# A transformer block on one core: the order of two engines at the start of the feed-forward's first pass, and a separate place for four loads of its last stage

## The chip, the cores and the metric

The kernel runs on one core of one Trainium2 chip. The core has a matrix engine (PE, with its weight loads PEld beside it), a vector engine (DVE), a scalar engine (ACT), a general engine (POOL) and SyncE (SP), which here only issues transfers (DMAs). Each engine takes its instructions in the order in which they are written and waits for the others by semaphores. The metric is the time of one execution on the device in microseconds (us), lower is better.

## The reference, cut to what matters

All inputs are float32; one sequence of 2048 rows of width 1024 passes through one block. The change lies in the second half of the block, the feed-forward, and at the boundary to it.

```python
def reference(x, c, w_cond, ..., w_out, g_ffn_pre, g_ffn_post, w_gate, w_up, w_down):
    ...                                   # attention and pooling give mix
    x = x + gate_m * rmsnorm(mix, g_mix_post)
    h = rmsnorm(x, g_ffn_pre) * (1.0 + scale_f) + shift_f
    f = (silu(h @ w_gate) * (h @ w_up)) @ w_down      # 1024 -> 2816 -> 1024
    return x + gate_f * rmsnorm(f, g_ffn_post)
```

## The kernel before, in words

Rows are held in 16 tiles of 128 rows, and the 2816 inner columns in 22 chunks of 128. A float32 product is made of three products of a rounded high part and a low part (`mm3`, L69 to L74: high by high on L72, the two mixed ones on L73 and L74). So an operand must be split before PE can use it: ACT casts the high part, DVE subtracts it from the operand and keeps the low part. In the down stage this is `split` (L62 on ACT, L63 on DVE). In the first passes it is `split_by_bank` (L1169 to L1177): ACT casts, ACT copies the rounded part to a PSUM bank (`rounded`), and DVE subtracts from there.

The feed-forward products are made by a scheme of seven products in place of eight (two levels for gate and up, one level for down). Four first passes p1 to p4 hold 11 blocks each. A block, `inner(q, j)`, has seven products with the names a, e, f, b, h, i and d, of six matmuls each. The order on PE is a, e, f, b, h, i of the first block, then a of the next, d of the first, e, f, b, h, i of the next, and so on. The weights of a block arrive as `g` and `u`; POOL makes the sums `s12` and `s34` of their parts; `g`, `s12`, `s34` and `u` are then split. Each of these splits, and each product, is a step with a number: e of the second block is step 8, its split of `s12` belongs to that step. What a product leaves in PSUM is taken up by DVE: `u2p` (L1410) from f, `p_c` (L1396) from b, `u3p` (L1418) from h, then `p_c` from e, from i and from d. Products d and e share two PSUM banks in turn (`e_ps`), so e of a block can only start when the `p_c` that reads the e of the block before has ended. `u4p` goes by ACT (L1406) and POOL (L1414).

While the first pass starts, the last tile of rows (number 15) still passes the boundary: DVE adds the input to it (L1272, 128x1024), ACT squares it and sums (L1255), DVE and POOL make the factor (`fr_v` L124, `fr_r` L126), and DVE and ACT scale one half each (`x1s`, L1266 and L1267). PE then transposes it (`f_pt`, L135) after h of the second block.

The order on PE, ACT, DVE and POOL is the order in which this loop writes the instructions; `n` counts the steps, `end_of_rows(n)` runs right after the products of a step, `split_up_to(n)` makes the splits of the steps ahead (up to six operand pairs), and `takes` are the DVE and ACT steps that take up results. SP's order is not written by hand: the compiler's scheduler places each transfer by when its tile is free. A transfer waits in SP's queue for all that stand before it.

The down stage works twice (`down(0)` and `down(1)`, for 1024 rows each) through the seven products p1, p2, p6, p7, p5, p4 and p3, each over 11 chunks, with 12 matmuls per chunk. The left operands (`g0p`, `g1p`) come from DRAM in groups of four chunks (three in p1), as two tiles of two chunks, and the groups take the pools `ring` and `fx` in turn; the right ones (`w0p`, `w1p`) come four chunks at a time. A tile can be loaded again when the splits of what it held are done. Products are split three chunks ahead, since there are six operand pairs. Results leave as `out_dram`; `x1b` and `cr` are the rows and first halves that are added at the end.

The tag `sr` names four tiles of 128x512 in pool `fx`. They serve the gate-and-up stage, and nothing uses them in the down stage.

## Time and profile before

| | |
|---|---|
| median of the runs, us | 2198.0 |
| lowest run, us | 2197.82 |
| profiled execution, us | 2196.93 |
| its span, us | 2195.1 |
| PE busy in the span | 99% |
| DVE, ACT, POOL busy | 76%, 62%, 55% |
| mean granted PE clock | 0.999 |

The span runs from the first to the last instruction of the profiled execution; 1.8 us of its time lie around it. The first pass starts at 983 us of the span, the first `down` at about 1767 us, and the second at 1976 us. A timeline row gives start and duration in us, engine, line, operation, out<-in, and in square brackets the idle time of the engine just before, with what ended it. PE's rows overlap: the next matmul starts before the one before has ended, so the pace is read from the starts.

### The profile page before, as it was taken

The numbers are of one execution on the slowest core, as the hardware profiler recorded it, in microseconds if no ns is written. First come the engines' busy times: TensorE is split into PE (matmuls) and PEld (weight loads), VectorE is DVE, ScalarE is ACT, GpSimd is POOL, SyncE is SP. The second block draws the span as 40 slices with busy tenths as digits, with TensorE's granted clock in tenths as the row PEclk, the third lists the DMA queues.
The fourth block names the chain that finished last, engine by engine and source line by source line (L and its number), as shares of the span: only waits on it lengthen the run. The fifth ranks groups of instructions, "written<-read, shape, count | busy, mean of one in ns | idle before, by whom it ended". The sixth has DMA issues, their size and how long they took to land.

```text
span 2195.1 us, 34256 instructions
## 1 busy us (share of the span) xinstructions
PE 2170.2 (99%) x10349; PEld 1795.4 (82%) x10349; DVE 1679.1 (76%) x2552; ACT 1356.9 (62%) x2796; POOL 1216.9 (55%) x1700
## 2 busy tenths in 40 slices
PE   8999999999999999999999999999999999999998
PEld 5888888888888888887888888888888888887887
DVE  7874499999999967647777878788778765576566
ACT  5335589989989855547666667654445444455454
POOL 1352277787879966537787877656666520032003
PEclk9999999999999999999999999999999999999999
DMA  9996886634343545668889989999999897589553
GB/s 315 338 294 208 284 215 177 172 90 120 111 137 95 154 163 199 218 197 284 285 299 314 310 267 293 292 327 327 304 300 303 304 333 256 196 261 316 187 198 118
DMA packets 365573, 524.78 MB, mean 239 GB/s; under 512 B 24198, under 2 KB 203978, under 8 KB 357836
## 3 DMA queue, kind: packets, MB, share of 16 engines
q1 hardware_dynamic: 360476, 518.13, 72.2%
q10 hardware_dynamic: 4912, 4.46, 0.7%
q8 instruction: 82, 1.34, 0.3%
q14 instruction: 103, 0.84, 0.1%
HBM read 350.01 MB, written 172.49 MB: 238 GB/s over the span
## 4 chain that ended last, share of the span: by engine, by line
PE 90%; DVE 4%; ACT 2%; POOL 2%; issue 1%; DMA 1%; SPq 0%; DVEq 0%; POOLq 0%; ACTq 0%
PE wt L964 4%; PE dn0p L74 3%; PE dn0p L72 3%; PE dn0p L73 3%; PE mix L74 3%; PE mix L72 3%; PE mix L73 3%; PE dn1p L73 2%; PE dn1p L72 2%; PE dn1p L74 2%; PE av L980 2%; PE z L929 2%; PE z L930 2%; PE av L979 2%; PE t_u L73 2%; PE t_g L73 2%
## 5 line engine op out<-in xcount | busy, mean ns | idle before, releaser
L953 POOL TENSOR_TENSOR w<-sg,pr 128x512 f32<-128x512 f32 (+2 forms) x320 | 306.6, 958 | 46.3 <-DVE pr L948 14.8
L948 DVE TENSOR_TENSOR_SCAN pr<-pr,carry,begin 128x512 f32<-128x512 f32 x192 | 244.0, 1271 | 0.0
L932 ACT ACTIVATE sg<-z 128x512 f32<-128x512 f32 (+2 forms) x320 | 183.1, 572 | 51.0 <-PE z L930 41.1
L63 DVE TENSOR_TENSOR wtl<-wt,wth 128x512 fp32r<-128x512 f32 (+1 forms) x320 | 189.5, 592 | 17.9 <-ACT wth L62 15.9
L62 ACT CAST wth<-wt 128x512 fp32r<-128x512 f32 (+1 forms) x320 | 181.8, 568 | 10.4 <-PE wt L964 8.1
L934 ACT ACTIVATE pr<-z 128x512 f32<-128x512 f32 (+2 forms) x320 | 182.1, 569 | 0.0
L964 PE MATMUL wt<-ident,w 128*128 128x128 f32 x1088 | 172.3, 273 | 1.6 <-POOL pr L944 1.1
L964 PEld LDWEIGHTS wt<-ident,w 128*128 128x128 f32 x1088 | 134.1, 140 | 32.8 <-POOL pr L944 1.9
L1493 ACT ACTIVATE sa<-sa 128x512 f32<-128x512 f32 x88 | 54.8, 632 | 164.7 <-DVE sa L1492 164.7
L979 PE MATMUL av<-wth,vt 128*128 128x512 f32 (+1 forms) x320 | 126.1, 394 | 0.9 <-ACT o L984 0.8
L63 DVE TENSOR_TENSOR g0p_l<-g0p,g0p_h 128x512 fp32r<-128x512 f32 x77 | 59.6, 774 | 79.7 <-ACT g0p_h L62 79.7
L72 PE MATMUL dn0p<-w0p_h,g0p_h 128*128 128x512 f32 x308 | 119.8, 389 | 0.0
L73 PE MATMUL dn0p<-w0p_l,g0p_h 128*128 128x512 f32 x308 | 119.8, 389 | 0.0
L74 PE MATMUL dn0p<-w0p_h,g0p_l 128*128 128x512 f32 x308 | 119.8, 389 | 0.0
L929 PE MATMUL z<-kt,qt 128*128 128x512 f32 (+2 forms) x320 | 118.7, 371 | 0.7 <-ACT pr L934 0.6
L980 PE MATMUL av<-wtl,vt 128*128 128x512 f32 (+1 forms) x320 | 117.8, 368 | 1.3 <-DVE wtl L63 1.2
L930 PE MATMUL z<-kt,qt 128*128 128x512 f32 (+2 forms) x320 | 116.9, 365 | 0.0
L72 PE MATMUL dn1p<-w1p_h,g1p_h 128*128 128x512 f32 x292 | 113.7, 389 | 0.6 <-ACT w1p_h L62 0.6
L73 PE MATMUL dn1p<-w1p_l,g1p_h 128*128 128x512 f32 x292 | 113.8, 390 | 0.3 <-DVE w1p_l L63 0.3
L74 PE MATMUL dn1p<-w1p_h,g1p_l 128*128 128x512 f32 x292 | 113.6, 389 | 0.0
L62 ACT CAST g0p_h<-g0p 128x512 fp32r<-128x512 f32 x77 | 48.0, 623 | 105.3 <-PE dn0p L73 89.3
L945 DVE TENSOR_TENSOR_SCAN pr<-pr,zero,begin 128x128 f32<-128x128 f32 (+3 forms) x128 | 111.1, 870 | 1.7 <-ACT pr L934 1.7
(852 smaller groups left out, 7155.9 us busy)
## 6 DMA issues: line engine op xcount, KB each, us to landing
pd<-p_c SPq DMA_DIRECT2D x176, 256.0 KB, 4.6
px<-pd SPq DMA_DIRECT2D x42, 1024.0 KB, 7.3
hs<-h2d SPq DMA_DIRECT2D x71, 256.0 KB, 4.8
wc<-in_w_cond_dram SPq DMA_DIRECT2D x32, 512.0 KB, 7.6
qt<-qd SPq DMA_DIRECT2D x64, 256.0 KB, 4.0
kt<-kd SPq DMA_DIRECT2D x96, 128.0 KB, 3.3
vt<-vd SPq DMA_DIRECT2D x48, 256.0 KB, 3.8
wd<-in_w_down_dram SPq DMA_DIRECT2D x44, 256.0 KB, 5.6
```

Source lines behind the costliest of these rows:

```text
L62: nc.scalar.copy(hi, src)
L63: low.tensor_tensor(lo, src, raw(hi), ALU.subtract)
L72: nc.tensor.matmul(ps, lh, rh, start=first and i == 0, stop=False)
L73: nc.tensor.matmul(ps, lh, rl, start=False, stop=False)
L74: nc.tensor.matmul(ps, ll, rh, start=False, stop=last and i == n - 1)
L929: nc.tensor.matmul(z[:, 0:L], qt[:, 0, i * P:(i + 1) * P], keys, start=True, stop=False)
L932: nc.scalar.activation(sg[:, 0:L], z[:, 0:L], AF.Sigmoid, scale=0.125)
L934: nc.scalar.activation(pr[:, 0:L], z[:, 0:L], AF.Sigmoid, scale=-0.125)
L948: nc.vector.tensor_tensor_scan(keys, keys, begin, carry, ALU.mult, ALU.bypass)
L953: nc.gpsimd.tensor_tensor(w[:, 0:L], sg[:, 0:L], pr[:, 1:L + 1], ALU.mult)
L964: nc.tensor.transpose(wt[:, i * P:(i + 1) * P], wss[u][i][:, b * P:(b + 1) * P], ident)
L979: nc.tensor.matmul(av[:, lo0:], vb, wh[:, lo0:], start=first, stop=False)
```

## The change

Three places are edited.

First, after step 1 of the main loop the splits are made up to and with step 8 before the last tile of rows is squared. So ACT's cast and copy of the second block's first `s12` and DVE's low part of it come ahead of the square and of what follows it.

Second, the scaling of the last tile of rows (with the closing of a pool and the opening of `ops0b`, which stand beside it) moves from `end_of_rows(4)` to the end of the body of step 5, behind the sums that take up b and e of the first block.

Third, in `down(1)` the first four chunks of the left operand of product p2 no longer go to the tiles of `ring` and `fx`, but to the four `sr` tiles, as four loads of 256 KB in place of two of 512 KB, and they are written eight steps ahead in place of five. Since this group no longer counts in the turn of the two pools, each later group of `down(1)` uses the other pool than before.

```diff
             def chunk(j):
                 name = f"{sb}{n}_{j}"
+                early = sb and n == "p2" and not j
 
                 def load_g():
                     m = min(QF, HF - held - j)
+                    if early:
+                        ph["gq", 0] = [ft("sr", f"g{name}_{i}") for i in range(m)]
+                        for i, t in enumerate(ph["gq", 0]):
+                            nc.sync.dma_start(t, ga[sb][a][:, i, :])
+                        return
                     quads.append(j)
                     ph["gq", j // QF] = t = raw_pair(ring if len(quads) % 2 else fx, f"g{name}", (P, 2, TB))
...
                 def split_gw():
                     pairs = []
-                    for kind, s in (("g", ph["gq", j // QF][j % QF // 2][:, j % QF % 2, :]), ("w", ph["w", j // 4][:, j % 4])):
+                    quad = ph["gq", j // QF]
+                    g = quad[j % QF] if len(quad) > 2 else quad[j % QF // 2][:, j % QF % 2, :]
+                    for kind, s in (("g", g), ("w", ph["w", j // 4][:, j % 4])):
...
                 if j % QF == 0:
-                    s.ahead.append((8 if begin else 5, load_g))
+                    s.ahead.append((8 if begin or early else 5, load_g))
...
     def end_of_rows(n):
         if n == 0:
             add_last_x(*last_rows)
-        if n == 4:
-            late.append((SEQUENCE[-1], last_scale[1](last_scale[2])))
-            op2st.close()
-            opools["0b"] = open_pool(h2st, "ops0b")
...
         if n == 1:
+            while split_to < 9:
+                steps[split_to].split()
+                split_to += 1
             last_scale.extend(ffn_rows(SEQUENCE[-1], *last_rows))
         if n == 3:
             last_scale.append(last_scale[0]())
+        if n == 5:
+            late.append((SEQUENCE[-1], last_scale[1](last_scale[2])))
+            op2st.close()
+            opools["0b"] = open_pool(h2st, "ops0b")
         next_side()
```

The order on PE and POOL stays as it was. Place one is DVE at the start of the first pass, right after the 128x1024 addition to the last rows (`x_15`); `p_1_g_l` and `p_1_s_l` are low parts of the second block's weights, `p_0_c` and the `u` names are what the first block's products leave. Before:

```order
L1177 TENSOR_TENSOR p_1_g_l<-p_1_321_13015,rounded 128x512
L1410 TENSOR_TENSOR u2p_0_13129<-fp_0_13113,p1p_0_13106 128x512
L1177 TENSOR_TENSOR p_1_s_l<-p_1_s_13087,rounded 128x512
L124 TENSOR_SCALAR fr_v<-s_15_13108 128x1
L1266 TENSOR_SCALAR x1s_13149<-x_15_13046,fr_r 128x512
L1396 TENSOR_TENSOR p_0_c_13157<-bp_0_13122,p1p_0_13106 128x512
L1418 TENSOR_TENSOR u3p_0_13173<-hp_0_13142,u2p_0_13129 128x512
L1396 TENSOR_TENSOR p_0_c_13175<-ep_0_13093,u3p_0_13173 128x512
```

And DVE at the same place with the change:

```order
L1177 TENSOR_TENSOR p_1_g_l<-p_1_321_13015,rounded 128x512
L1177 TENSOR_TENSOR p_1_s_l<-p_1_s_13087,rounded 128x512
L1410 TENSOR_TENSOR u2p_0_13135<-fp_0_13119,p1p_0_13106 128x512
L124 TENSOR_SCALAR fr_v<-s_15_13114 128x1
L1396 TENSOR_TENSOR p_0_c_13149<-bp_0_13128,p1p_0_13106 128x512
L1418 TENSOR_TENSOR u3p_0_13165<-hp_0_13142,u2p_0_13135 128x512
L1396 TENSOR_TENSOR p_0_c_13167<-ep_0_13093,u3p_0_13165 128x512
L1266 TENSOR_SCALAR x1s_13169<-x_15_13046,fr_r 128x512
```

The low part of `s12` moved one place ahead of `u2p`, and the scaling `x1s` moved from ahead of the three sums on b, h and e to behind them. ACT at the same place, as one piece of the difference, from the copy of the first block's product a (`p1p_0`) on; `m` and `s_15` are what the square writes:

```order
 L1401 COPY p1p_0_13106<-ap_0_13078 128x512
-L1255 ACTIVATE m_11480,s_15_13108<-x_15_13046 128x1024
-L1406 COPY u4p_0_13120<-ep_0_13093 128x512
 L1169 CAST p_1_s_h<-p_1_s_13087 128x512
 L1176 COPY rounded<-p_1_s_h 128x512
-L1267 ACTIVATE x1s_13149<-x_15_13046,fr_r 128x512
-L1169 CAST p_1_s_h<-p_1_s_13110 128x512
+L1255 ACTIVATE m_11480,s_15_13114<-x_15_13046 128x1024
+L1406 COPY u4p_0_13126<-ep_0_13093 128x512
+L1267 ACTIVATE x1s_13169<-x_15_13046,fr_r 128x512
+L1169 CAST p_1_s_h<-p_1_s_13116 128x512
```

On ACT the cast and the copy of `s12` moved ahead of the square and of `u4p`. Place two is SP's queue late in product p1 of `down(1)`, with the loads for p2 (`g1p2`, `w1p2`; the number behind is the first chunk). Before:

```order
L1788 DMA w1p2_0_23890<-in_w_down_dram 128x4x512
L1870 DMA x1b0_3cu_23879<-x1d3_107 128x512
L1873 DMA cr3_23883<-f0d3_153 128x512
L1780 DMA g1p2_0_320_23886<-ga1a12_144 128x1024
L1780 DMA g1p2_0_321_23887<-ga1a12_144 128x1024
L1903 DMA out_0_dram<-y0_u1_22149 128x512
L1903 DMA out_0_dram<-cr1_23685 128x512
L1903 DMA out_0_dram<-y0_u2_22150 128x512
L1903 DMA out_0_dram<-cr2_23823 128x512
L1780 DMA g1p2_4_320_23986<-ga1a12_144 128x1024
```

And with the change:

```order
L1794 DMA w1p2_0_23894<-in_w_down_dram 128x4x512
L1878 DMA x1b0_3cu_23887<-x1d3_107 128x512
L1881 DMA cr3_23891<-f0d3_153 128x512
L1911 DMA out_0_dram<-y0_u1_22149 128x512
L1911 DMA out_0_dram<-cr1_23685 128x512
L1786 DMA g1p2_4_320_23990<-ga1a12_144 128x1024
L1911 DMA out_0_dram<-y0_u2_22150 128x512
L1911 DMA out_0_dram<-cr2_23831 128x512
L1786 DMA g1p2_4_321_23991<-ga1a12_144 128x1024
```

The two loads of p2's first group are gone from here, and the first load of its second group (`g1p2_4`) stands ahead of two of the stores that it stood behind. SP's queue is rearranged at the start of the first pass too: the loads of the weights of block 3 and three stores `pd` of the first block now stand ahead of two loads for later passes (`y_raw` and `hs` from `h2d`), which stood ahead of them. Place three is where the first group's loads now stand in SP's queue, two at the end of the gate-and-up stage and, in these rows, two during p1 of `down(0)`:

```order
L1786 DMA g0p2_4_321_22095<-ga0a12_137 128x1024
L1781 DMA g1p2_0_2_23798<-ga1a12_144 128x512
L1781 DMA g1p2_0_3_23799<-ga1a12_144 128x512
L1878 DMA x1b1_4cu_24051<-x1d12_116 128x512
L1786 DMA g0p2_0_320_22004<-ga0a12_137 128x1024
L1794 DMA w0p2_4_22098<-in_w_down_dram 128x4x512
L1786 DMA g0p2_0_321_22005<-ga0a12_137 128x1024
L1878 DMA x1b1_4s_24052<-x1d12_116 128x512
L1878 DMA x1b1_5cu_24096<-x1d13_117 128x512
```

Before, the three loads `x1b1_4cu`, `x1b1_4s` and `x1b1_5cu` stood between `g0p2_4_321` and `g0p2_0_320`; two of them have moved behind `g0p2_0_321`, and two new loads of the same size, 256 KB, stand there.

## The prediction

> **What bounds the kernel now.** The page's busy times come first, then the list of PE's waits (who is waited for, total us, times, longest).

> ```profile
> PE 2170.2 (99%) x10349; PEld 1795.4 (82%) x10349; DVE 1679.1 (76%) x2552; ACT 1356.9 (62%) x2796; POOL 1216.9 (55%) x1700
> ...
> PE ep L72 <- DVE p_c L1396: 2.1, 1, 2.1
> ...
> PE dn1p L72 <- ACT w1p_h L62: 0.6, 1, 0.6
> ...
> PE dn1p L73 <- DVE w1p_l L63: 0.3, 1, 0.3
> ```

> PE is busy for 99% of the span, so a microsecond counts only where PE stands still or runs slower. Three rows of the list lie where the change is. The first is one wait of 2.1 us of product e on a sum by DVE; the other two, 0.6 and 0.3 us, belong to a `down(1)` product. PE's timeline shows what the first costs.

> ```profile
> 990.05 0.39 PE L72 MATMUL ip<-v14p1h,p_u_h 128*128 128x512 f32 x1
> ...
> 993.90 0.39 PE L74 MATMUL dp<-y22p,p_s_l 128*128 128x512 f32 x1
> 996.37 0.47 PE L72 MATMUL ep<-v14p1h,p_s_h 128*128 128x512 f32 x1 [2.08 <-DVE p_c L1396]
> ...
> 1001.48 0.39 PE L72 MATMUL bp<-yap1h,p_g_h 128*128 128x512 f32 x1
> ```

> From the first matmul of i to the last of d there are 17 steps (i, a and d have six each): 3.85 / 17 = 0.2265 us from start to start at full pace. So e of the second block was due at 993.90 + 0.23 = 994.13. The row at 1001.48 is the fourth matmul of b, the 16th after 993.90 (six of e, six of f, four of b). It was due at 993.90 + 16 x 0.2265 = 997.52 and came 3.96 us late. That is more than the wait. The windows of 1 us say why (the number after POOL's is the granted clock):

> ```profile
> 997.00:998.00 1.00, 1.00 (x6) 0.77 (x5) 1.00 (x3) 0.49 (x1) 0.00 (x0) 0.88 0.89 287
> 998.00:999.00 1.00, 1.00 (x4) 0.81 (x3) 0.95 (x2) 0.66 (x3) 0.00 (x0) 0.50 0.86 300
> 999.00:1000.00 1.00, 1.00 (x3) 0.73 (x3) 0.00 (x0) 0.97 (x3) 0.00 (x0) 0.50 0.89 256
> 1000.00:1001.00 1.00, 1.00 (x4) 0.79 (x3) 0.80 (x2) 0.97 (x3) 0.00 (x0) 0.50 0.41 120
> 1001.00:1002.00 1.00, 1.00 (x6) 0.82 (x5) 1.00 (x2) 0.68 (x2) 0.36 (x1) 0.91 0.96 294
> ...
> 2006.00:2007.00 1.00, 0.42 (x2) 0.19 (x1) 0.90 (x2) 1.00 (x3) 0.00 (x0) 1.00 1.08 432
> ```

> About 1.3 us after PE resumed, its clock fell to half and stayed there for some 3.4 us: 0.12 + 0.50 + 0.50 + 0.50 + 0.09 = 1.71 us lost, beside 2.25 us of wait and restart. In the second place the clock stayed at 1.00 through the short waits:

> ```profile
> 2005.67 0.39 PE L74 MATMUL dn1p<-w1p_h,g1p_l 128*128 128x512 f32 x1
> 2006.64 0.50 PE L72 MATMUL dn1p<-w1p_h,g1p_h 128*128 128x512 f32 x1 [0.58 <-ACT w1p_h L62]
> 2007.45 0.50 PE L73 MATMUL dn1p<-w1p_l,g1p_h 128*128 128x512 f32 x1 [0.31 <-DVE w1p_l L63]
> ...
> 2014.41 0.39 PE L72 MATMUL dn1p<-w1p_h,g1p_h 128*128 128x512 f32 x1
> ...
> 2005.45 0.62 ACT L62 CAST g1p_h<-g1p 128x512 fp32r<-128x512 f32 x1 [5.21 <-DMA g1p<-ga1a]
> ...
> 1991.20 0.46 SPq L1788 DMA_DIRECT2D w1p<-in_w_down_dram  x1
> ...
> 1997.63 0.86 SPq L1780 DMA_DIRECT2D g1p<-ga1a  x2
> ```

> The row at 2014.41 is the 31st after 2005.67, due at 2005.67 + 31 x 0.2265 = 2012.69: 1.72 us late, a little of it in the following chunk. ACT stood for 5.21 us until the group loaded at 1997.63 had landed; w's cast follows behind it.

> **The change, part by part: the first pass.** How e's wait arose is read on three engines:

> ```profile
> 986.51 0.74 POOL L1367 TENSOR_TENSOR p_s<-p_s,p 128x256 f32<-128x256 f32 x1
> ...
> 987.11 0.58 ACT L1401 COPY p1p<-ap 128x512 f32<-128x512 f32 x1
> 989.07 1.06 ACT L1255 ACTIVATE m<-x 128x1024 f32<-128x1024 f32 x1 [1.38 <-DVE x L1272]
> ...
> 991.25 0.59 ACT L1176 COPY rounded<-p_s_h 128x512 f32<-128x512 f32 x1
> ...
> 988.96 0.68 DVE L1177 TENSOR_TENSOR p_g_l<-p,rounded 128x512 fp32r<-128x512 f32 x1
> ...
> 991.94 0.69 DVE L1177 TENSOR_TENSOR p_s_l<-p_s,rounded 128x512 fp32r<-128x512 f32 x1 [1.70 <-ACT rounded L1176]
> ...
> 993.35 0.95 DVE L1266 TENSOR_SCALAR x1s<-x,fr_r 128x512 f32<-128x512 f32 x1 [0.66 <-POOL fr_r L126]
> 994.23 0.68 DVE L1396 TENSOR_TENSOR p_c<-bp,p1p 128x512 f32<-128x512 f32 x1
> 994.83 0.67 DVE L1418 TENSOR_TENSOR u3p<-hp,u2p 128x512 f32<-128x512 f32 x1
> 995.54 0.69 DVE L1396 TENSOR_TENSOR p_c<-ep,u3p 128x512 f32<-128x512 f32 x1
> ...
> 990.77 1.29 POOL L1414 TENSOR_TENSOR u4p<-u4p,u2p 128x512 f32<-128x512 f32 x1 [1.14 <-ACT u4p L1406]
> ...
> 992.77 0.55 POOL L126 TENSOR_TENSOR fr_r<-fr_v,mhalf 128x1 f32<-128x1 f32 x1 [0.70 <-DVE fr_v L124]
> ```

> DVE stood twice, 1.70 us for ACT's copy behind the square and 0.66 us for the row's factor, and the sum that frees e's bank ended at 995.54 + 0.69 = 996.23. With the change ACT is idle where it waited 1.38 us for the square's input: `s12` is ready at 987.25, the copy `p1p` ends at 987.69, so cast (0.62, as in the ACT row of 2005.45) and copy (0.59) end by about 988.95, before the square can start at 989.07. The square loses nothing. DVE keeps `p_g_l` at 988.96, then has 0.60 us from start to start (994.23 to 994.83): `p_s_l` 989.56, `u2p` 990.16, `fr_v` 990.76, the sum on b 990.85, `u3p` 991.45, the sum on e 992.15, as 0.70 passed from `u3p` to it. It ends at 992.84, **1.3 us before PE comes to e** at 994.13. The wait goes, and with it the idle time ahead of the half clock: 3.96 us.

> The change adds a wait behind the sums: `x1s` needs `fr_r`. POOL's `u4p` starts with `u2p` done at 990.84 in place of 990.77, ends at 992.13, and `fr_r` at 992.7, so `x1s` starts at 992.75, where DVE is free anyway. Queued behind it are the sum on i and the low part for h of the second block, which PE reaches at 994.13 + 18 x 0.2265 = 998.2. ACT's half of `x1s` takes 0.7 us, the cast and copy 1.2 us: ready by 994.7, the low part by 995.4. 2.8 us are spare.

> What is late next is e of the third block:

> ```profile
> 1004.18 1.36 DVE L143 TENSOR_SCALAR f_h<-f_pt,af,bf 128x128 f32<-128x128 f32 x4 [1.11 <-PE f_pt L135]
> ...
> 1006.50 0.69 DVE L1396 TENSOR_TENSOR p_c<-ep,u3p 128x512 f32<-128x512 f32 x1
> ...
> 1008.10 0.39 PE L72 MATMUL ep<-v14p1h,p_s_h 128*128 128x512 f32 x1
> ```

> Before, its bank was free at 1007.19, 0.91 us ahead. PE is to come there 3.96 us earlier, at 1004.14. DVE cannot gain all of that: it had 1.11 us idle before `f_h`, and ACT and DVE run ahead of the old trace by 0.6 us (`x1s` at 992.75 for 993.35) to about 1.5 us (where ACT no longer waits for PE's late e). With that 1.11 us of slack used up, the sum ends 1.7 to 2.6 us earlier than it did, at 1004.6 to 1005.5, and as early as 1004.1 if what DVE lost to late products between `x1s` and `f_h` comes back too. So the new wait lies between 0 and 1.3 us; I take **0.3**, near the low end, because PE's products, for which DVE's sums stood then, are all in PSUM 2 to 4 us sooner. It is short of the 2.08 us that went ahead of the half clock. The first edit is worth 3.96 - 0.3 = **3.65 us** (2.65 to 3.96).

> On SP the first block's stores and block 3's weights go ahead of `y_raw` and `hs`. These two serve the second and third pass, the nearer one by step 34 or so, 26 steps of 1.36 us after this e; no cost. Block 3's weights come sooner.

> **The change: the down stage.** With its first group in `sr` long before, ACT can cast p2's chunk 0 when it fell idle, at 2005.45 - 5.21 = 2000.24: two casts to 2001.5, two low parts to about 2002.9, 3.0 us before PE's 2005.90. Both waits and what followed them go: **1.72 us**. The cover is w's group, issued at 1991.20. If it landed only with g's, the gain would be nothing; the cast of w followed g's without a wait of its own, which doesn't tell. It was issued 6.4 us before g, and I take the full gain.

> The second group, now in the other pool, stands ahead of two stores, so it comes sooner. The four early loads cost two more issues. In `down(0)`'s p1 they hold the place of two `x1b` loads of the same size; at the end of gate and up they stand ahead of right operands for p1's last chunks, eight chunks of 12 x 0.2265 = 2.7 us away. What one load can delay is bounded by the listed landing of twice its size:

> ```profile
> g1p<-ga1a SPq DMA_DIRECT2D x14, 512.0 KB, 5.3
> ```

> Two of them, at most 5.3 us each, stay under 8 x 2.7 = 21.7 us. No cost.

> **The sum** is 3.65 + 1.72 = 5.37 us. Against the profiled execution's own 2196.93 us (span 2195.1, 1.8 us around it) that gives 2191.6; the median of the runs, 2198.0, stands 1.07 higher, which gives **2192.6**.

> **The rivals.** *The clock is not tied to the wait.* If the half clock would come in this stretch without 2.08 us idle, 1.71 us of the gain stay away: 2192.6 + 1.7 = 2194.3. Against it: with waits of 0.58 and 0.31 us the clock stayed at 1.00, and the half clock stands right behind the longest idle time of the pass. [...] I give it 0.08.

> *DVE and ACT become the bound after e* (0.12): the new waits reach 1.3 us or come at two products: 2192.6 + 1 to 2.5 = 2193.6 to 2195.1.

> *One edit doesn't do what it says* (0.12): if w's group holds p2 back, 2192.6 + 1.7 = 2194.3; if another result frees e's bank last, 2198.0 - 1.7 = 2196.3. Both failing, 2198.0 (0.03).

> *Slower: ACT's own transfers.* ACT issues block 5's weights itself and waited there for a store of weight sums:

> ```profile
> 1015.03 0.40 ACTq L1351 DMA_DIRECT2D p<-in_w_up_dram  x1
> 1015.47 0.62 ACT L1169 CAST p_s_h<-p_s 128x512 fp32r<-128x512 f32 x1 [1.06 <-DMA tdt<-wd]
> ...
> 1022.19 0.39 PE L72 MATMUL hp<-v32p1h,p_s_h 128*128 128x512 f32 x1
> ```

> Behind it is the cast for h of block 3. From 1015.47 cast, copy and low part take some 2.3 us, so h at 1022.19 had 4.4 us to spare. PE now comes 3.65 us earlier; if the store lands no earlier, 0.8 us are left. PE waits for whatever comes above that, and above 2 us it pays 1.71 us of half clock too. To eat 5.37 us the wait must reach 3.7, so the store must land 4.5 us later than before, beyond 1019.5; at 7 us later the time is 2200.5. Against it: POOL, which makes the sums, gains with block 3's weights. 0.03.

> **How the numbers follow.** The forecast holds 0.62, its own range 2191.3 to 2193.6 (no new wait, 2198.0 - 5.68 = 2192.3, and 1 us for the runs; 1.3 us of it, 2193.6). The rivals hold 0.08, 0.12, 0.12, 0.03 and 0.03. The range takes in all but the last two; its low end is the profiled execution's 2196.93 - 5.68 = 2191.3, less the 0.9 us by which it lies under the lowest run: 2190.5 to 2196.5. Over 2% is 44 us, about what a measurement of this kernel can tell from no change; no case comes near, which leaves 0.01 for faster, 0.97 for the same and 0.02 for slower.

> **What would show it.** In the new profile PE's list has no row of e on `p_c` above 1 us and none of `dn1p` on `w1p`; the granted clock is 1.00 in every microsecond between 990 and 1005; DVE's 1.70 us wait ahead of `p_s_l` is gone; ACT's wait of 5.21 us for `g1p` at the start of p2 is gone. The prediction is wrong if e still waits for another bank or operand, if the half clock stays, or if PE's saved time comes back as waits of e or h in blocks 2 to 5.

## The result

The changed kernel takes 2193.95 us (median of 22 runs), the kernel before 2197.32 us (median of 22 runs beside them). The ratio is 0.9984, with a 95% interval of 0.9978 to 0.9991: 3.4 us less, by the interval 2.0 to 4.8. That is far inside the 2% that was called no change. The forecast was 2192.6 us, with a range of 2190.5 to 2196.5; it was built on a median of 2198.0 us from three runs of the kernel before.

The profiled execution of the changed kernel has a span of 2192.6 us, 2.5 us less than the one before. PE's waits in the stages that the change touches (who is waited for, total us, times, longest):

```profile
PE ep L72 <- ACT p_u_h L1169: 0.9, 1, 0.9
PE ep L72 <- ACT p_g_h L1169: 0.8, 1, 0.8
...
PE ap L72 <- DVE u2p L1410: 0.5, 1, 0.5
...
PE ep L72 <- DVE p_c L1396: 0.2, 1, 0.2
```

The 2.1 us wait of e on `p_c` is gone, and so are both rows of `dn1p` on `w1p`, with ACT's wait of 5.21 us for `g1p` (its longest between 1985 and 2015 is now 2.36 us). But four waits stand there that the kernel before did not have. DVE's and PE's timelines of the changed kernel at the old place:

```profile
989.29 0.68 DVE L1177 TENSOR_TENSOR p_s_l<-p_s,rounded 128x512 fp32r<-128x512 f32 x1
...
991.93 0.69 DVE L1396 TENSOR_TENSOR p_c<-ep,u3p 128x512 f32<-128x512 f32 x1
992.55 0.95 DVE L1266 TENSOR_SCALAR x1s<-x,fr_r 128x512 f32<-128x512 f32 x1
...
993.66 0.39 PE L74 MATMUL dp<-y22p,p_s_l 128*128 128x512 f32 x1
993.88 0.39 PE L72 MATMUL ep<-v14p1h,p_s_h 128*128 128x512 f32 x1
...
997.00:998.00 1.00, 1.00 (x6) 0.81 (x6) 0.53 (x1) 0.97 (x3) 0.00 (x0) 1.00 0.51 147
```

The low part comes without a wait, the sum on e ends at 992.62, 1.26 us before PE needs the bank, and the granted clock is 1.00 in this microsecond, where it fell before, and in the four behind it. How far PE leads the old trace is read from pairs of starts of the same matmul, first of before, then of after (the row of e of the third block has its partner, 1008.10, in the prediction):

```profile
981.49 1.91 PE L135 MATMUL f_pt<-ident,xr 128*128 128x128 f32 x16
1002.17 0.39 PE L72 MATMUL hp<-v32p1h,p_s_h 128*128 128x512 f32 x1
1301.41 0.39 PE L72 MATMUL ap<-yap4h,p_g_h 128*128 128x512 f32 x1
2186.91 0.39 PE L74 MATMUL dn1p<-w1p_10h,g1p_10l 128*128 128x512 f32 x1
```

```profile
981.24 1.91 PE L135 MATMUL f_pt<-ident,xr 128*128 128x128 f32 x16
997.96 0.39 PE L72 MATMUL hp<-v32p1h,p_s_h 128*128 128x512 f32 x1
1004.15 0.47 PE L72 MATMUL ep<-v14p1h,p_s_h 128*128 128x512 f32 x1
1300.75 0.39 PE L72 MATMUL ap<-yap4h,p_g_h 128*128 128x512 f32 x1
2184.52 0.39 PE L74 MATMUL dn1p<-w1p_10h,g1p_10l 128*128 128x512 f32 x1
```

PE leads by 0.25 us ahead of the first pass, 4.21 at h of the second block, 3.95 at e of the third, 0.66 where the fourth pass begins, 2.39 at the end. So the first edit won 4.21 - 0.25 = 3.96 us where it acts, the down stage 2.39 - 0.66 = 1.73, and in between 3.55 us were lost again. 0.26 us of it went at e of the third block. The places of the rest are PE's new waits (wait and slower restart together cost 1.28 us at the first, 0.44 at the second, 1.57 at the last two):

```profile
1024.84 0.47 PE L72 MATMUL ep<-v14p1h,p_s_h 128*128 128x512 f32 x1 [0.85 <-ACT p_u_h L1169]
1120.50 0.47 PE L72 MATMUL ep<-v14p2h,p_s_h 128*128 128x512 f32 x1 [0.17 <-DVE p_c L1396]
1289.99 0.47 PE L72 MATMUL ap<-yap3h,p_g_h 128*128 128x512 f32 x1 [0.49 <-DVE u2p L1410]
1293.83 0.47 PE L72 MATMUL ep<-v14p3h,p_s_h 128*128 128x512 f32 x1 [0.83 <-ACT p_g_h L1169]
```

Behind the first of them stands ACT, held by its own two transfers (the ACT rows, then DVE's row with the sum that frees e's bank):

```profile
1012.10 0.38 ACTq L1351 DMA_DIRECT2D p<-in_w_gate_dram  x1
1013.95 0.40 ACTq L1351 DMA_DIRECT2D p<-in_w_up_dram  x1
1014.39 0.62 ACT L1169 CAST p_s_h<-p_s 128x512 fp32r<-128x512 f32 x1 [3.81 <-PE dp L73]
...
1015.66 0.69 DVE L1177 TENSOR_TENSOR p_s_l<-p_s,rounded 128x512 fp32r<-128x512 f32 x1 [2.35 <-ACT rounded L1176]
...
1024.00 0.69 DVE L1396 TENSOR_TENSOR p_c<-ep,u3p 128x512 f32<-128x512 f32 x1
```

ACT stood for 3.81 us, DVE for 2.35 behind it, and in DVE's order the sum on e ends at 1024.69, just ahead of PE's start at 1024.84. The same sum stood here in the trace of before:

```profile
1025.38 0.69 DVE L1396 TENSOR_TENSOR p_c<-ep,u3p 128x512 f32<-128x512 f32 x1
```

It ended at 1026.07, and PE came to e at 1027.63, 1.56 us later. Now PE leads by 3.95 us when it comes there, but the sum by only 1.38, since ACT's cast behind the loads has moved by 1.08 us alone (1015.47 to 1014.39). Behind the last two waits stand POOL, SP and DVE:

```profile
1271.92 5.34 POOL L1577 TENSOR_TENSOR wd<-wd 128x512 f32<-128x512 f32 x4
1273.26 4.35 SPq L1592 DMA_DIRECT2D tdt<-wd  x4
...
1285.31 0.69 DVE L1396 TENSOR_TENSOR p_c<-ip,u3p 128x512 f32<-128x512 f32 x1 [4.06 <-DMA pd<-p_c]
```

POOL makes four weight sums in a row, SP stores each as it comes, the stores of DVE's results stand behind them, and DVE then waits 4.06 us for a stored tile. That wait isn't new. In the trace of before it cost PE nothing:

```profile
1286.01 0.69 DVE L1396 TENSOR_TENSOR p_c<-ip,u3p 128x512 f32<-128x512 f32 x1 [3.70 <-DMA pd<-p_c]
```

Now DVE leads by 0.7 us there and PE by 2.2.

### The profile page after: what moved, and what is told of

It is laid out like the page before. It is cut to its first block, busy times and chain, and to the rows that moved or that the text cites. A ratio compares the mean times of both kernels' runs of the same rounds, so it can differ in the third digit from the quotient of the medians.

```text
span 2192.6 us, 34258 instructions
## 1 busy us (share of the span) xinstructions
PE 2168.6 (99%) x10349; PEld 1795.0 (82%) x10349; DVE 1681.2 (77%) x2552; ACT 1356.7 (62%) x2796; POOL 1219.1 (56%) x1700
## 3 DMA queue, kind: packets, MB, share of 16 engines
q8 instruction: 82, 1.34, 0.3%
## 4 chain that ended last, share of the span: by engine, by line
PE 89%; DVE 5%; ACT 2%; POOL 2%; issue 1%; DMA 1%; DVEq 0%; SPq 0%; ACTq 0%; POOLq 0%
PE wt L964 4%; PE dn0p L72 3%; PE dn0p L73 3%; PE dn0p L74 3%; PE dn1p L72 3%; PE dn1p L73 3%; PE dn1p L74 3%; PE mix L74 3%; PE mix L73 3%; PE mix L72 3%; PE av L980 2%; PE z L929 2%; PE z L930 2%; PE av L979 2%; PE t_u L74 2%; PE t_g L74 2%
## 5 line engine op out<-in xcount | busy, mean ns | idle before, releaser
L63 DVE TENSOR_TENSOR wtl<-wt,wth 128x512 fp32r<-128x512 f32 (+1 forms) x320 | 189.4, 592 | 18.0 <-ACT wth L62 15.9
L62 ACT CAST wth<-wt 128x512 fp32r<-128x512 f32 (+1 forms) x320 | 181.8, 568 | 10.6 <-PE wt L964 8.2
L63 DVE TENSOR_TENSOR g0p_l<-g0p,g0p_h 128x512 fp32r<-128x512 f32 x77 | 59.6, 774 | 79.8 <-ACT g0p_h L62 79.8
L72 PE MATMUL dn0p<-w0p_h,g0p_h 128*128 128x512 f32 x308 | 119.8, 389 | 0.0
L73 PE MATMUL dn0p<-w0p_l,g0p_h 128*128 128x512 f32 x308 | 119.8, 389 | 0.0
L74 PE MATMUL dn0p<-w0p_h,g0p_l 128*128 128x512 f32 x308 | 119.8, 389 | 0.0
L72 PE MATMUL dn1p<-w1p_h,g1p_h 128*128 128x512 f32 x292 | 113.6, 389 | 0.0
L73 PE MATMUL dn1p<-w1p_l,g1p_h 128*128 128x512 f32 x292 | 113.6, 389 | 0.0
L74 PE MATMUL dn1p<-w1p_h,g1p_l 128*128 128x512 f32 x292 | 113.6, 389 | 0.0
L62 ACT CAST g0p_h<-g0p 128x512 fp32r<-128x512 f32 x77 | 48.0, 623 | 105.4 <-PE dn0p L73 89.3
## 6 DMA issues: line engine op xcount, KB each, us to landing
wc<-in_w_cond_dram SPq DMA_DIRECT2D x32, 512.0 KB, 7.6
```

What stands on the lines that cost most here:

```text
L62: nc.scalar.copy(hi, src)
L63: low.tensor_tensor(lo, src, raw(hi), ALU.subtract)
L72: nc.tensor.matmul(ps, lh, rh, start=first and i == 0, stop=False)
L73: nc.tensor.matmul(ps, lh, rl, start=False, stop=False)
L74: nc.tensor.matmul(ps, ll, rh, start=False, stop=last and i == n - 1)
```

## The experiments

In all of them the lead is counted as above, in us over the profiled execution of before and from `f_pt` on. This table holds one profiled execution each; the columns from "end of pass 1" to "end of pass 3" show what the three passes left of it (that of pass 2 is read at e of its last block, 1189.57 in the trace of before).

```
                     h of      end of    end of    end of    PE's last
                     block 2   pass 1    pass 2    pass 3    matmul
changed kernel        3.96      2.42      1.98      0.41      2.14
first_only            3.96      3.05      0.48     -0.76     -0.85
down_only             1.62      0.70     -0.46     -0.39      1.34
split_only            2.15      1.78     -0.33     -0.01      0.02
scale_only            3.25      2.10     -0.57     -0.39     -0.05
load5_sync            3.96      3.56      3.29      1.92      3.64
sums_later            3.96      3.06      1.67      1.99      3.72
load5_early           3.96      2.03      1.13      0.77      2.49
load5_sums_later      3.96      1.39     -0.06      0.26      1.99
load5_sums_apart      3.96      2.13      0.59     -2.52     -0.79
sum_x4                2.80      1.21     -1.68     -1.36      0.37
sum_x6                1.32      0.94      0.21     -0.34      1.38
sum_x11              -4.39     -4.40     -6.14     -7.30     -5.57
```

**The parts apart.** The first pass alone (the diff without the part in `down`):

> The two edits of the first pass alone, the down stage as before. Theory (the lead is won and then handed back): e of block 2 starts without a wait and the clock stays at 1.00, so PE leads the old trace by about 4.2 us at h of block 2; waits of e in block 5 of the first pass (about 1.1 us), of e in the second pass (0.4) and of a and e in the third pass (1.6) hand it back, and the two waits of dn1p on w1p (0.58 and 0.31 us) are there again. That leaves 0.7 us of span: about 2196.6 us against 2197.3 before. Rival (the waits behind e come from the early loads of the down stage or from a changed order of their tiles): the 4.2 us last, no new wait in the three passes, 2193.1 to 2193.6 us.

Measured: 2195.80 us, before 2196.94, ratio 0.9995 (0.9986 to 1.0004). e of block 2 starts without a wait, the 3.96 us are there, and both waits of `dn1p` are back, where the lead stays as it was (-0.76 to -0.85). In the passes 4.7 us are lost, partly at places of their own:

```profile
1177.41 0.47 PE L72 MATMUL ap<-yap2h,p_g_h 128*128 128x512 f32 x1 [1.07 <-DVE u2p L1410]
...
2008.74 0.51 PE L72 MATMUL dn1p<-w1p_h,g1p_h 128*128 128x512 f32 x1 [0.67 <-ACT w1p_h L62]
```

So the new waits do not come from the early loads of the down stage. The down stage alone (the diff's part in `down`, the main loop as before):

> The four early loads of the down stage alone, the first pass as before. Theory: both waits of dn1p on w1p go and nothing else moves; 1.7 us less than before, 2195.6 us, with e of block 2 waiting 2.1 us and the half clock behind it as before, and none of the new waits in the passes. Rival (the early loads delay other loads and cause the new waits): new waits of e or a appear in the first or third pass, and less than 1 us is left of the gain.

Measured: 2197.61 us against 2196.94, ratio 0.9996 (0.9987 to 1.0006), where 2195.6 was expected; the interval doesn't tell 1.7 us from nothing. In its trace the step at p2 is 1.34 + 0.39 = 1.73 us, as in the changed kernel. The surprise is in the first pass, where the order is that of before:

```profile
994.02 0.39 PE L74 MATMUL dp<-y22p,p_s_l 128*128 128x512 f32 x1
996.49 0.47 PE L72 MATMUL ep<-v14p1h,p_s_h 128*128 128x512 f32 x1 [2.08 <-DVE p_c L1396]
...
997.00:998.00 1.00, 1.00 (x6) 0.80 (x5) 1.00 (x3) 0.47 (x2) 0.00 (x0) 1.00 0.81 279
...
2190.00:2191.00 1.00, 0.00 (x0) 0.00 (x0) 0.11 (x1) 0.00 (x0) 0.00 (x0) 0.55 0.73 272
```

The same wait of 2.08 us, and the clock stays at 1.00. It therefore leads before by 1.62 us at block 2 without any edit there. It also loses 2.0 us in the passes, so that loss is no consequence of the changed order alone. The two edits of the first pass one by one (`while split_to < 9` alone, then the move of the scaling alone):

> Of the first pass only the low part ahead of the square; the row is scaled where it was, ahead of the sums. By the rows of before, the sum on e then ends at about 995.6 and e of block 2 waits some 1.5 us instead of 2.1. Theory (half clock follows idle time of 2.08 us and not of 0.58; 1.5 lies between): the clock tells on which side 1.5 us falls. If half clock stays, the gain is 0.6 us in the first pass; if it goes, 2.3 us. Rival (the half clock belongs to this stretch and not to the wait): half clock for about 3.4 us in 995 to 1001 whatever the wait.

> Of the first pass only the row scaled behind two sums; the square stays ahead of the low part, so DVE keeps its 1.70 us wait. By the rows of before, the sum on e ends 1.5 us sooner, at about 994.7, and e of block 2 waits some 0.5 to 0.6 us. Theory: no half clock behind so short a wait (none came behind 0.58 us elsewhere), so this edit alone wins about 3.2 of the 3.96 us at e of block 2, before the later passes hand part of it back; 2195 to 2196.5 us. Rival (half clock belongs to the stretch): 1.7 us less of it.

Measured: 2197.34 us, ratio 1.0003 (0.9994 to 1.0011), and 2196.47 us, ratio 0.9997 (0.9988 to 1.0006). PE's rows at e of block 2, of the first and of the second kernel:

```profile
996.95 0.50 PE L72 MATMUL ep<-v14p1h,p_s_h 128*128 128x512 f32 x1 [1.50 <-DVE p_c L1396]
```

```profile
996.45 0.47 PE L72 MATMUL ep<-v14p1h,p_s_h 128*128 128x512 f32 x1 [0.45 <-DVE p_c L1396]
```

Waits of 1.50 and 0.45 us, as worked out, and a clock of 1.00 behind both, so that at block 2 they lead before's trace by 2.15 and 3.25 us. Each edit takes its share off the wait, and only both together take all of it.

**The clock.** Two kernels lengthen the sum that frees e's bank:

```
-            nc.vector.tensor_tensor(t, ps, rest, ALU.add)
+            for _ in range(6 if m == 0 and kind and sb else 1):
+                nc.vector.tensor_tensor(t, ps, rest, ALU.add)
```

> The changed kernel with the sum that frees e's bank for block 2 done four times in a row instead of once (three more sums of 0.65 to 0.70 us, the same result). The sum then ends at about 994.6 to 994.7, and e of block 2 waits some 0.7 to 1.0 us. Theory (half clock follows an idle time near 2 us, not one below 1): the granted clock stays at 1.00 in each microsecond up to 1002. Rival (any wait here does it): half clock for 3.4 us.

> The changed kernel with the sum that frees e's bank for block 2 done six times in a row (five more sums). It ends at about 996.0, and e of block 2 waits some 2.0 to 2.4 us, as before the change but for another reason. Theory (the half clock follows the idle time, whatever causes it): half clock for about 3.4 us, 1 to 2 us behind the restart, and 1.7 us lost to it. Rival (the half clock had to do with the square, the row's scaling or the transfers of that moment, or needs an idle time of 3.4 us): the clock stays at 1.00.

With four sums e waited 0.90 us and the clock stayed (2197.57 us, one run). With six it waited longer than before the change, and the clock stayed too (2197.86 us, one run), against the theory:

```profile
996.35 0.39 PE L74 MATMUL dp<-y22p,p_s_l 128*128 128x512 f32 x1
999.09 0.47 PE L72 MATMUL ep<-v14p1h,p_s_h 128*128 128x512 f32 x1 [2.35 <-DVE p_c L1397]
...
1001.00:1002.00 1.00, 1.00 (x6) 0.81 (x5) 1.00 (x2) 0.66 (x2) 0.00 (x0) 1.00 0.91 336
...
2192.00:2193.00 1.00, 0.00 (x0) 0.00 (x0) 0.40 (x1) 0.00 (x0) 0.00 (x0) 0.73 0.44 166
```

So the theory was changed: the clock is judged in stretches that run on by themselves. A last kernel with eleven sums made the wait too long to be missed:

> The changed kernel with the sum that frees e's bank for block 2 done eleven times in a row. Five more sums than in the run with six, at 0.65 to 0.70 us each: e of block 2 waits 5.6 to 5.9 us. Theory (the clock is judged in stretches of 3.4 us that run on by themselves, and falls behind a stretch in which PE stood for more than about half; at the end of ten runs it fell 1.9 to 5.0 us after PE's last matmul): a wait of 2.1 or 2.35 us lies in one stretch or is cut in two, by chance, which is why one run of three showed the half clock; a wait above 5.0 us can't be missed, and half clock begins 1.9 to 5.0 us behind the start of the wait and lasts 3.4 us or 6.8 us in all, of which PE feels what lies behind its restart. Rival (the half clock seen in the first profile had nothing to do with PE's wait): the clock stays at 1.00 here too.

```profile
994.68 0.39 PE L74 MATMUL dp<-y22p,p_s_l 128*128 128x512 f32 x1
1001.04 0.77 PE L72 MATMUL ep<-v14p1h,p_s_h 128*128 128x512 f32 x1 [5.98 <-DVE p_c L1397]
...
998.00:999.00 1.00, 0.00 (x0) 0.00 (x0) 0.94 (x2) 0.00 (x0) 0.00 (x0) 0.82 0.63 242
1005.00:1006.00 1.00, 1.00 (x5) 0.79 (x4) 0.26 (x1) 0.97 (x3) 0.00 (x0) 0.76 0.34 99
...
2196.00:2197.00 1.00, 0.00 (x0) 0.00 (x0) 1.00 (x3) 0.00 (x0) 0.94 (x2) 0.86 0.93 348
```

The wait is 5.98 us (5.6 to 5.9 expected). A share of 0.82 in a microsecond that goes from 1.0 to 0.5 puts the fall at 998.64, 3.6 us after PE stopped; the 0.76 puts the rise at 1005.48, 6.84 us later. Both lie within what was expected. The time was 2203.14 us (one run).

At the end of the trace, after PE's last matmul, the clock falls once more, at 2196.72, 1198.08 us after the first fall. In the trace of before, read in windows of 0.02 us, the half clock went from 997.76 to 1001.17, 3.413 us, and the clock fell again at 2192.42. The two falls lie 1194.66 us apart, 350 x 3.4133 us (349 or 351 stretches would be 3.423 or 3.404 us long), and the 1198.08 us with eleven sums are 351 x 3.4133. So the beat held through both executions, and the fall at the end tells where the stretches lay at e of block 2. In the trace with six sums the end fall is at 2192.46 (the 0.73 above) and a border, 350 stretches ahead of it, at 997.79, which cuts the wait from 996.74 to 999.09 into 1.05 and 1.30 us. In `down_only` the 0.55 above puts it at 2190.10 and a border at 995.43, which cuts the wait from 994.41 to 996.49 into 1.02 and 1.06. In `split_only`, whose end fall at 2191.97 puts a border at 997.30, the whole 1.50 us lay in one stretch, 44% of it, and the clock stayed. In the trace of before the stretch from 994.35 to 997.76 held the wait to 996.37: 2.02 us, 59%, and the clock fell. In that with eleven sums the stretch behind the fall, to 1002.05, held the wait to 1001.04, 70%, and the half clock went on for a second stretch.

**The places where the lead is lost.** Block 5's loads by SP in place of ACT, and the last group of weight sums two steps later:

```
-                (nc.scalar if m in (1, 4, 5) else nc.sync).dma_start(
+                (nc.scalar if m in (1, 4) else nc.sync).dma_start(
```

```
-DOWN_AT = (10, 26, 42, 58, 74, 106, 130, 156, 172, 188, 204)
+DOWN_AT = (10, 26, 42, 58, 74, 106, 130, 156, 172, 188, 206)
```

> The changed kernel with one word different: the two loads of block 5's weights are issued by SP, not by ACT. Theory (ACT, held 3.8 us by its own two transfers at 1012 to 1014, makes DVE's low part and the sum on e late): ACT's wait of 3.81 us ahead of the cast for h of block 3 goes, e of block 5 starts without its 0.85 us wait, and PE's lead over before stays 1.1 us larger to the end of the first pass. What of it lasts to the end depends on the third pass: if its waits are set by transfers at fixed times, they grow by as much and the time stays at 2194.0; if not, 2192.8. Rival (DVE's own work is the limit there): the wait at e of block 5 stays above 0.5 us.

> The changed kernel with the last group of weight sums of the down stage two steps later in the third pass (206 in place of 204). Theory (the third pass's waits of a and e come from four weight sums in a row on POOL, 5.3 us, whose four stores stand on SP ahead of the stores that free DVE's result tiles): only two of the sums and their stores stand there now, DVE's 4.1 us wait for a stored tile falls below 2 us, and the waits of a (0.49) and e (0.83) near 1290 go; 1.3 to 1.6 us less, 2192.4 to 2192.7 us. Rival (the transfers themselves are full there): the waits stay within 0.3 us of what they were and the time at 2194.0.

The first: 2195.26 us against 2197.05, ratio 0.9990 (0.9981 to 0.9999). e of block 5 no longer waits and 3.56 us of the lead reach the end of the first pass, as the theory has it; in the third pass 1.4 of them go at the same two products as in the changed kernel. The time is not below the 2194.0 us of the changed kernel, where 2192.8 or 2194.0 was expected. The second: 2193.93 us against 2197.05, ratio 0.9984 (0.9976 to 0.9993). In its third pass PE has no wait, and DVE's longest there is a third of what it was:

```profile
1273.62 1.69 SPq L1592 DMA_DIRECT2D tdt<-wd  x2
...
1283.44 0.69 DVE L1396 TENSOR_TENSOR p_c<-ip,u3p 128x512 f32<-128x512 f32 x1 [1.25 <-DMA pd<-p_c]
```

So both causes are shown in the traces. The time is that of the changed kernel, though, and not the 2192.4 to 2192.7 us expected: the profiled execution lost 1.4 us in the second pass. Three more kernels follow, in which ACT issues block 5's loads four steps sooner, and the weight sums are put later (206 as above) or apart:

```
-        r[0].ahead = [({1: 9, 2: 12}.get(m, 16 if q == 3 else 14), load)
+        r[0].ahead = [({1: 9, 2: 12, 5: 18}.get(m, 16 if q == 3 else 14), load)
...
-            for n, op in zip((0, 6, 7, 8, 9), down_sums(i)):
+            for n, op in zip((0, 6, 7, 8, 9) if k < 106 else (0, 6, 8, 10, 12), down_sums(i)):
```

> The changed kernel with block 5's two loads issued by ACT four steps (5.4 us) earlier, at about 1005 to 1006, where SP issues nothing and no store of weight sums is due. Theory (ACT was held at 1012 to 1014 because its two transfers had to wait for stores and a store of weight sums issued just ahead): ACT's wait of 3.81 us there goes, e of block 5 starts with less than 0.3 us of wait, and by the end of the first pass PE has kept at least 3.4 of the 3.96 us won at e of block 2 (the changed kernel kept 2.4). Rival (the waits at block 5 come from DVE's and POOL's own work): a wait of 0.3 to 0.9 us stays. The end depends on the third pass, whose waits this doesn't touch: 2193 to 2194.5 us.

> The changed kernel with block 5's loads four steps earlier and the last group of weight sums two steps later: both cures together. Theory (the lead is taken back at a few places, each with a cause of its own): from the first block's products to the end of the third pass PE keeps about 3 us of the 3.96, where the changed kernel kept 0.4 and either cure alone 1.9 to 2.0; 2192 to 2193 us, what chance waits in the second pass leave of it. Rival (the transfers of the three passes as a whole set their length): what one cure wins is lost at the next place, no more than 2.0 us are kept, and the time is that of the one cure alone, 2193.9.

> The changed kernel with block 5's loads four steps earlier and the weight sums of the last six groups of the down stage spread over twice the steps (6, 8, 10, 12 in place of 6, 7, 8, 9 steps behind their load). Theory (four sums in a row on POOL and their four stores on SP delay the stores that free DVE's result tiles, in the second pass at 1177 to 1181 as in the third at 1290 to 1297): waits of a and e at both places go or fall below 0.3 us, and 3 us or more of the 3.96 are kept to the end of the third pass; 2191.5 to 2193 us. Rival (the longer hold of the one tile for weight sums delays the next load of weights, and POOL's own sums for PE come later): new waits, time at 2194 us or above.

Measured against 2197.44 us of before: 2194.85 us, ratio 0.9991 (0.9982 to 1.0000); 2194.75 us, 0.9991 (0.9982 to 0.9999); 2198.94 us, 1.0004 (0.9995 to 1.0013). All three miss in the first pass, and the row of ACT in the first of them says why, with SP's row beside it and PE's behind:

```profile
1011.27 0.38 ACTq L1351 DMA_DIRECT2D p<-in_w_up_dram  x1
1011.69 0.59 ACT L1406 COPY u4p<-ep 128x512 f32<-128x512 f32 x1 [3.35 <-DMA tdt<-wd]
...
1009.18 0.32 SPq L1592 DMA_DIRECT2D tdt<-wd  x1
...
1016.28 0.47 PE L72 MATMUL ep<-v14p1h,p_s_h 128*128 128x512 f32 x1 [1.30 <-ACT p1p L1401]
```

The second load goes out only at 1011.27, after a store of weight sums that SP itself issues at 1009.18. The two share no tile by name. By the semaphores in the trace, the load waited for the transfer that had used its semaphore last: here that store, landed at 1011.25, 0.02 us ahead of it; in the changed kernel the store issued at 1010.64, landed at 1013.92, 0.03 us ahead of the load at 1013.95. Written earlier, the second load waits for an earlier store, but longer: 2.9 us from ACT's last work on, where in the changed kernel it went out 1.5 us behind the first load. ACT is held for 3.35 us in all (3.81 in the changed kernel), now ahead of work for e of block 4, and that e pays 1.2 to 1.9 us in the three kernels. Spreading the sums brings PE waits at other products and loses 3.1 us from the last e of the second pass on (0.59 to -2.52). The kernel with both cures has no wait in the third pass, as `sums_later` has none. No version is measurably faster than the changed kernel.

## Why the prediction was right, and where it was not

- **The edit of the first pass** did what was worked out: the sum on e 1.26 us ahead (1.3 forecast), the row's scaling at 992.55 (992.75), 3.96 us won at h of block 2, the loss at e of the third block 4.21 - 3.95 = 0.26 us (0.3).
- **The down stage**: 1.72 or 1.73 us for 1.72, in each of the ten traces of the table that have the edit. The three without it move by -0.09 to 0.34 us in this stage, since the two waits differ from execution to execution (0.29 and 0.30 us in `scale_only`); the edit is worth 1.4 to 1.8 us.
- **The size that failed is the sum, 5.37 us against 3.4 measured (2.0 to 4.8).** Two of its terms were wrong. The first is the 1.71 us of half clock, booked as a sure part of the wait. The clock does follow the wait, so the rival that denied it falls with `sum_x11`, but a wait of 2.08 us brings the half clock only if a border doesn't cut it into parts that are too short, as the 1.02 and 1.06 us in `down_only`. At the end of the trace of before, 1.71 us (by chance the same figure) lay between PE's last matmul and the border at 2189.01; this share of 50% left the clock, which fell one stretch later. The changed kernel's end, where it fell 1.95 us after PE's last matmul, shows that 57% is enough. Between these bounds a wait of 2.08 us meets the half clock in 47 to 61 of 100 executions (an estimate: the free part of 3.41 us, 1.33, plus twice the 0.13 to 0.37 us by which the wait exceeds 1.95 or 1.71, over 3.41), which makes it 0.8 to 1.0 us on the average.
- **The second is the loss in the passes, booked at nothing** beyond e of the third block. The changed kernel lost 3.55 us from h of block 2 to the end of the third pass. The prediction had the mechanism at block 5, ACT behind its own transfers, as the rival for slower, but looked at h, which had time to spare, and not at e, whose sum stands behind the same low part in DVE's order. The third pass, where DVE's wait for a stored tile was already 3.70 us long, was not looked at.
- **How much of that loss the change causes stays open.** Kernels that led by 3.96 us lost 2.0 to 4.7, `load5_sums_apart` 6.5; those that led by less, or lagged, lost 1.7 to 4.2, down_only among them, with the old order. The profiled execution of before had no new wait there, so it flattered the passes as it overcharged the clock. The table splits it in part. In the first pass the loss goes with a lead: `sum_x11`, which lagged, lost nothing there, and the eight kernels that led, with block 5's loads as they were, lost 0.4 to 1.6 us. In the second and third pass `sum_x11` lost 2.9 us without a lead. With one trace for each kernel, the loss there can't be split between the lead and the chance of an execution. By the medians it is smaller than in the one trace: of the 2.0 us that the gain fell short, the clock takes 0.7 to 0.9, which leaves 1.1 to 1.3 for the passes (an estimate, with the measured interval of 1.4 to either side).
- "The time comes back as waits of e or h in blocks 2 to 5" was named as what would make the prediction wrong. It happened in part, 1.5 us to the end of the first pass (3.96 to 2.42), too little to leave the range.
- **Part of the hit is luck.** The gain was 2.0 us short, the time only 1.35 us off, because the median of before came out 0.7 us lower with more runs; and the range of 6 us took in most of the rivals.

## What to carry to other kernels

A gain is worth what is left of it at the end of the stage: follow the lead over the old trace, product by product, and ask at each place where the old trace had no wait how much time it had to spare. A single profiled execution can hold a chance event (here 1.71 us of half clock) and miss others; before a figure of a few microseconds goes into a sum, see whether a second trace of the same code shows it. The loads that ACT issues here held it for up to 3.81 us, as long as they had to wait for other transfers, and writing them four steps earlier didn't help: the second then stood 2.9 us for another store, with other work of ACT behind it.

## What the runs showed of the hardware

```profile
2192.00:2193.00 1.00, 0.00 (x0) 0.00 (x0) 0.00 (x0) 0.00 (x0) 0.00 (x0) 0.71 1.03 381
```

```profile
2186.00:2187.00 1.00, 0.00 (x0) 0.00 (x0) 0.99 (x2) 0.97 (x4) 0.08 (x1) 0.93 0.92 340
```

That is 5.13 us and 1.95 us after PE's end; the other twelve traces lie between, at 2.12 to 4.70 us. The spread of 3.2 us is nearly one stretch, which fits a beat without regard to the kernel. Behind a stretch in which PE was idle for 59% (at e of block 2 in before) or 57% (at the end of the changed kernel) the clock fell; behind 50% (at the end of before) and 44% (in `split_only`) it did not.

Time that the view calls busy can be followed by half clock too. In the traces of `first_only` and `split_only` the clock fell for one stretch at 24.6 and 24.5 us of the span, and again at 48.5 and 48.4 us; those of before, the changed kernel, `down_only`, `scale_only` and `sum_x11` have no such fall. These four falls, too, lie whole numbers of stretches (635 and 628) ahead of the fall at the end. They come before the first pass, so the leads above don't hold them; the execution times do. The rows of `first_only`:

```profile
46.14 1.86 PE L613 MATMUL am_columns<-ones,acc 128*128 128x1 f32 x16
...
48.00:49.00 1.00, 1.00 (x4) 0.80 (x5) 0.93 (x4) 0.56 (x1) 0.00 (x0) 0.75 0.00 0
```

PE was busy for all of the stretch from 45.08 to 48.49, but for 1.86 us of it with matmuls of one column. If these count as idle time, 54% was idle ahead of this fall, which lies between the bounds above; but a stretch of the changed kernel, from 19.41 to 22.83, kept the clock with 58% by this count. No run varies these matmuls, so this is not shown. From 60 us on to PE's last matmul these seven traces hold some 4360 stretches. The clock fell only at e of block 2, in before and with eleven sums, and in no other stretch was PE idle for more than 44%.
